# Second layer's MLA gate: tiles 2 to 5 as two more pairs of seven block products, and the products of all pairs collected in PSUM

## The chip, the cores and the metric

The kernel runs on one core of one Trainium2 chip. The metric is the device time of one execution in microseconds; its median is taken over several runs.

## The reference, cut to what matters

A hybrid decoder of two layers works on 512 tokens of width 1024, ahead of which 16 meta tokens are put (528 positions). Each layer projects once, runs two mixers beside each other (causal pooling, latent attention with 8 heads), and gates both:

```python
h = rmsnorm(h_res, norm_gain[l])
proj = h @ w_in[l]
u_pool, z_pool, c_q, c_kv, k_rope, z_mla, g_pool, g_mla = jnp.split(proj, IN_SPLIT_POINTS, axis=-1)
y_pool = (pool_mix(u_pool, pool_w_group[l], pool_scale[l]) * jax.nn.silu(z_pool)) @ pool_w_up[l]
o_mla = mla(c_q, c_kv, k_rope, pos, ...)
y_mla = (o_mla * jax.nn.silu(z_mla)) @ mla_w_up[l]
merged = jax.nn.sigmoid(g_pool) * y_pool + jax.nn.sigmoid(g_mla) * y_mla
h_res = h_res + merged @ w_out[l]
```

The change lies in `g_mla` and `g_pool` of the second layer: two products of 1024 x 1024 weights with the 1024 x 512 normed input. In the second layer the meta tokens are no longer needed there.

## The kernel before, in words

**Layout and matmuls.** Activations lie with features on the 128 partitions and tokens along the row, so an output tile is 128 features by 512 tokens. A float32 product is made as three matmuls (`mm3`, L192, L195, L196): high part of the weights by high part of the activations, high by low, low by high. Weights come in blocks of 128 x 512 (four 128 x 128 weights): `wload` lets SyncE load a block into one of three `raw` buffers (L115), ScalarE makes the high part `whi` (L187) and VectorE the low part `wlo` (L188), of which there are three each. The loads run a few blocks ahead of TensorE. The activations' parts are `hh` and `hl`, one pair for each of the eight slices of 128 features.

**Order.** `plan` is a list of products in program order, and `stream` issues them block by block and stops after every six matmuls. In the attention of a layer each of 8 heads has 4 gaps; `gap` calls `fill(FILL[l], RESERVE[l])`, which issues planned products until a clock of estimated times is FILL ns further on, or until the product named by RESERVE is done; the rest comes after the heads. So the gate products stand between the score, transpose and `p @ v` matmuls of the heads. `after(ns, fn)` issues something once that clock has gone on by ns.

**Gate products of the second layer.** `g_mla` is made as eight plain tiles gm0 to gm7: 8 slices x 3 matmuls of 512 columns, then `ev_gate`: ScalarE's tanh out of PSUM, and for tiles 0 to 5 a store to DRAM (L1069, from ScalarE's queue), since their place in SBUF is still in use; `gates_again` loads them later. `g_pool` is made as four pairs of tiles gp0 to gp3 by `fast`, a scheme of the Strassen kind: two tiles by 512 tokens in seven products of 512 x 128 weights with 256 tokens, each 4 slices x 3 matmuls of 256 columns. Product 1 takes the first tile's weights of the first 512 features, 2 those of the second 512, 4 the second tile's of the second 512; 3, 5, 6 and 7 take sums of weights. `weight_sums` has made these sums in DRAM: for a pair four copies by SyncE (L356, each held behind a matmul that is 14 us old by the clock) and four adding DMAs by GpSimd (L359, behind one of 4 us). For the pool gate that is done in the first layer. The activations' sums and differences for products 4 to 7 are made by `mixed` between the heads (in the names below `cq` for products 6 and 5, `sq` for 7 and 4).

A pair uses four of the PSUM buffers `mm` (there are four in all): products 1 and 2 share one, 7 and 4 one, 5 and 3 one, 6 has its own. A product that shares adds onto what is there. In `fast`, product 1 is copied by ScalarE into half of an `sv` buffer (L632), and five operations of VectorE (L634, L636, L638, L644, L647) combine the products:

```python
order = (1, 6, 7, 5, 2, 4, 3)
...
key = {1: "a", 2: "a", 6: "b", 7: "c", 4: "c", 5: "d", 3: "d"}[p]
...
mm3(ps, w[0][:, c:c + P], w[1][:, c:c + P], xh, xl, k == 0 and p not in (2, 4, 3), k == 3, True)
```

`got_gp` applies the tanh to each of the four half tiles (ScalarE, L657) and VectorE multiplies it onto the pooling branch's `am`. The plan's order is gm0, gm1, gp0, gm2, gp1, gm3, gp2, gm4, gp3, gm5, gm6, gm7; gm6 and gm7 are kept for after the heads.

**Elsewhere.** The rope of the query halves is done by GpSimd and VectorE together (L539 on VectorE, then L541 and L542 on GpSimd). The output stage makes its own seven products with ScalarE copies (L1163).

## Time and profile before

| What | Value |
|---|---|
| runs | 782.56, 782.64, 784.69 us |
| median | 782.64 us |
| profiled execution | 782.78 us, its span 781.0 us |
| TensorE matmul (PE) | 774.8 us, 99% |
| TensorE weight load (PEld) | 712.5 us, 91% |
| VectorE (DVE) | 568.6 us, 73% |
| ScalarE (ACT) | 445.2 us, 57% |
| GpSimd (POOL) | 233.3 us, 30% |
| DMA | 112.92 MB, 145 GB/s on the mean |

Times are in microseconds from the span's start. A row of the timeline gives start, duration, engine, line of the kernel, operation, output and inputs, and the number of instructions; what stands in square brackets is the idle time ahead of it and what ended it. A row of a group gives the count, the busy time, the mean ns of one, and the idle time before them with its releasers. A row of the windows table gives a stretch's length and each engine's busy time in it. The weight loads overlap the matmuls on TensorE.

### The profile page before, as it was taken

To read this page: it belongs to the slowest core of one execution; us is meant where nothing else is said; L and a number is where in the kernel's file an instruction comes from. 1 tells how busy PE (TensorE), PEld (TensorE's weight loads), DVE (VectorE), ACT (ScalarE), POOL (GpSimd) and SP (SyncE) were. 2 spreads that over 40 slices of the span, in tenths; PEclk is the share of its full clock that TensorE was granted. 3 is DMA by queue.
4 is the path that set the end of the run, shared out by engine and by line. 5 is a ranking of instruction groups with operands and counts; after the bars stand their busy time and mean duration, and the time that the engine had idled before them with its cause. 6 is when DMAs were issued, how large, how long until landed. Compare 5 with 4: busy or idle time off the path is not lost.

```text
span 781.0 us, 15326 instructions
## 1 busy us (share of the span) xinstructions
PE 774.8 (99%) x5469; PEld 712.5 (91%) x5469; DVE 568.6 (73%) x1326; ACT 445.2 (57%) x1016; POOL 233.3 (30%) x303
## 2 busy tenths in 40 slices
PE   9999999999999999999999999999999999999998
PEld 9999899999999999999997898887788999988887
DVE  5848787446778876589764477865897888864984
ACT  7645555645566665645564356546667766664462
POOL 1024525103335333211330136221006625440213
PEclk9999999999999999999999999999999999999999
DMA  6242467765746465565662524425556666662655
GB/s 244 82 97 89 124 170 151 179 167 144 156 109 165 115 141 120 155 168 175 168 170 81 98 87 123 132 63 181 141 140 162 174 174 166 176 221 75 209 154 138
DMA packets 65325, 112.92 MB, mean 145 GB/s; under 512 B 10704, under 2 KB 15696, under 8 KB 65248
## 3 DMA queue, kind: packets, MB, share of 16 engines
q1 hardware_dynamic: 55344, 92.18, 40.0%
q0 software_dynamic: 8896, 17.92, 13.0%
q10 hardware_dynamic: 1008, 1.84, 0.6%
q8 instruction: 43, 0.70, 0.4%
q14 instruction: 34, 0.28, 0.1%
HBM read 100.18 MB, written 22.62 MB: 157 GB/s over the span
## 4 chain that ended last, share of the span: by engine, by line
PE 92%; DVE 3%; DMA 2%; ACT 1%; issue 1%; SPq 0%; DVEq 0%; ACTq 0%
PE mm L192 26%; PE mm L196 26%; PE mm L195 26%; PE S L192 3%; PE S L196 2%; PE S L195 2%; PE mm L979 2%; PE o L985 1%; PE o L984 1%; DVE wlo L188 1%; PE S L506 1%; DMA raw<-win 1%; PE mm L408 1%; DMA raw<-wsum 1%; PE mm L465 0%
## 5 line engine op out<-in xcount | busy, mean ns | idle before, releaser
L192 PE MATMUL mm<-hh,whi 128*128 128x264 f32 (+2 forms) x992 | 307.0, 312 | 0.1
L196 PE MATMUL mm<-hh,wlo 128*128 128x264 f32 (+2 forms) x992 | 304.7, 309 | 0.3 <-DVE wlo L188 0.2
L195 PE MATMUL mm<-hl,whi 128*128 128x264 f32 (+2 forms) x992 | 304.4, 308 | 0.0
L188 DVE TENSOR_TENSOR wlo<-raw,whi 128x512 fp32r<-128x512 f32 (+1 forms) x253 | 179.8, 714 | 103.7 <-ACT whi L187 101.2
L187 ACT ACTIVATE whi<-raw 128x512 fp32r<-128x512 f32 (+1 forms) x253 | 154.2, 612 | 166.4 <-PE mm L195 105.0
L192 PEld LDWEIGHTS mm<-hh,whi 128*128 128x128 f32 x992 | 186.6, 189 | 11.0 <-ACT racc L993 0.5
L195 PEld LDWEIGHTS mm<-hl,whi 128*128 128x128 f32 x992 | 187.2, 189 | 8.7
L196 PEld LDWEIGHTS mm<-hh,wlo 128*128 128x128 f32 x992 | 186.2, 188 | 9.4 <-DVE wlo L188 1.1
L922 POOL TENSOR_SCALAR pa<-pa,rs 128x272 f32<-128x272 f32 (+1 forms) x32 | 33.0, 1031 | 103.0 <-DVE rs L941 64.2
L922 POOL TENSOR_SCALAR cq<-cq,rs 128x400 f32<-128x400 f32 (+1 forms) x32 | 52.2, 1631 | 0.0
L192 PE MATMUL mm<-cq,whi 128*128 128x264 f32 (+2 forms) x140 | 43.8, 313 | 0.0
L195 PE MATMUL mm<-cq,whi 128*128 128x264 f32 (+2 forms) x140 | 43.7, 312 | 0.0
L196 PE MATMUL mm<-cq,wlo 128*128 128x264 f32 (+2 forms) x140 | 43.3, 312 | 0.1
L908 DVE CUSTOM_DVE_ANT_0 S<-S,maskw,nqs 128x272 f32<-128x272 f32 (+4 forms) x80 | 38.6, 497 | 5.2 <-PE S L196 4.9
L725 POOL TENSOR_TENSOR racc<-racc,tmp 128x264 f32<-128x264 f32 (+1 forms) x15 | 14.5, 964 | 84.9 <-ACT tmp L724 84.8
L304 DVE TENSOR_TENSOR tl<-mm,th 128x512 fp32r<-128x512 f32 (+1 forms) x64 | 30.0, 482 | 8.0 <-ACT th L303 6.3
L359 POOL DMA_DIRECT2D wsum<-wout x8 | 7.0, 873 | 91.7 <-PE mm L196 77.0
L303 ACT ACTIVATE th<-mm 128x512 fp32r<-128x512 f32 (+1 forms) x64 | 26.2, 432 | 10.2 <-PE mm L979 9.6
L915 ACT ACTIVATE cq<-S,bia 128x400 f32<-128x400 f32 (+2 forms) x48 | 24.4, 513 | 13.2 <-DVE bia L953 8.5
L192 PE MATMUL mm<-u,whi 128*128 128x264 f32 (+1 forms) x96 | 31.3, 326 | 0.0
L196 PE MATMUL mm<-u,wlo 128*128 128x264 f32 (+1 forms) x96 | 30.9, 322 | 0.0
L195 PE MATMUL mm<-kn,whi 128*128 128x264 f32 (+1 forms) x96 | 30.6, 320 | 0.0
(344 smaller groups left out, 1684.2 us busy)
## 6 DMA issues: line engine op xcount, KB each, us to landing
raw<-win SPq DMA_DIRECT2D x139, 256.0 KB, 2.9
raw<-wout SPq DMA_DIRECT2D x22, 256.0 KB, 3.5
bc<-kdr SPq DMA_DIRECT2D x16, 264.0 KB, 4.6
wsum<-wout SPq DMA_DIRECT2D x16, 256.0 KB, 3.5
raw<-wpu SPq DMA_DIRECT2D x16, 256.0 KB, 3.2
wsumgp<-win SPq DMA_DIRECT2D x16, 256.0 KB, 3.3
raw<-wmu SPq DMA_DIRECT2D x16, 256.0 KB, 2.8
raw<-wsumgp SPq DMA_DIRECT2D x16, 256.0 KB, 3.6
```

The source lines that it names most:

```text
L187: act.activation(hi[:, :n], raw[:, :n], AF.Copy)
L188: dve.tensor_sub(lo[:, :n], raw[:, :n], hi[:, :n].bitcast(F32))
L192: first = pe.matmul(out, wh, xh, start=start, stop=False, skip_group_check=more)
L195: pe.matmul(out, wh, xl, start=False, stop=False, skip_group_check=more)
L196: newest[0] = pe.matmul(out, wl, xh, start=False, stop=stop, skip_group_check=more)
L303: act.activation(hi[:, a:b], src, AF.Copy)
L304: dve.tensor_sub(lo[:, a:b], src, hi[:, a:b].bitcast(F32))
L725: self.acc_last = gp.tensor_add(self.acc[:, a:b], self.acc[:, a:b], t[:, :b - a])
L908: dve.tensor_tensor_reduce(out=sv, in0=sv, in1=mask, scale=nqs[:, i, h:h + 1], scalar=3e38, op0=ALU.add, op1=ALU.min, accum_out=bia[:, c:c ...
L915: act.activation(pv, sv, AF.Exp, scale=-1.0, bias=bia[:, i:i + 1], accum_out=rs[:, c:c + 1])
L922: gp.tensor_scalar(pt[i], pt[i], rs[:, i:i + 1], None, op0=ALU.mult)
L979: pe.transpose(tr[:, P * (i - j):P * (i - j + 1)], pt[i][:, NM + P * j:NM + P * (j + 1)], ident)
```

## The change

1. Tiles 2 and 3 of `g_mla` become the pair gq1, tiles 4 and 5 the pair gq2, by `fast` with the evacuation `got_gm`: tanh by halves and a store of each half. `weight_sums` makes their sums in the second layer from the query products on, one of its 16 steps every 4000 ns of the clock (four copies on SyncE and four adding DMAs on GpSimd for each pair).
2. In `fast` the products come in the order 1, 2, 6, 7, 5, 4, 3. Products 1, 6, 5 and 3 add up in one PSUM buffer, 7 and 4 in another, 2 has a third. ScalarE copies the buffer to `sv` after products 1, 6 and 7 (`keep`); VectorE combines once after 2, 5 and 4; 3 is taken from PSUM directly. A pair takes two `sv` buffers. In `mixed` a sign changes with it.
3. The plan's order becomes gm0, gm1, gp0, gq1, gp1, gp2, gq2, gp3, gm6, gm7; FILL of the second layer goes from 2700 to 2640, and RESERVE names gp3 there.

```diff
@@ line 50 of before @@
 G_H, G_CKV, G_CQ, G_QN, G_QR, G_KN, G_KR, G_PS = 0, 8, 10, 16, 17, 18, 19, 20
 N_GAIN = 24
 
-FILL = (2950.0, 2700.0)
-RESERVE = ("gm5", "gm5")
+FILL = (2950.0, 2640.0)
+RESERVE = ("gm5", "gp3")
 LAG = 2000.0
 SPL = 240
 RET = 12500.0
@@ line 335 of before @@
     ksr = [dp.tile([H, T], F32, name=f"ksr{l}") for l in range(DEPTH)]
     kdr = [dp.tile([H, T], F32, name=f"kdr{l}") for l in range(DEPTH)]
 
-    wsum = {n: [dp.tile([P, 4, 512], F32, name=f"wsum{n}{u}") for u in range(k)] for n, k in (("gp", 4), (0, 2), (1, 2))}
+    wsum = {n: [dp.tile([P, 4, 512], F32, name=f"wsum{n}{u}") for u in range(k)] for n, k in (("gp", 4), ("gm", 3), (0, 2), (1, 2))}
     gate = dp.tile([P, 6, SEQ], F32, name="gate")
 
     hbuf = [(slot(f"hh{k}", F32R), slot(f"hl{k}", F32R)) for k in range(8)]
@@ line 344 of before @@
     XH = [(NM, NM + N2), (NM + N2, T)]
     (a, b), (_, c) = XH
 
-    def weight_sums(name, w):
+    def weight_sums(name, w, u0=0):
         def made(u, i):
             a, b = w[2 * u], w[2 * u + 1]
             d = wsum[name][u]
@@ line 358 of before @@
         def add(d, src):
             behind(gp.dma_start(d, src[1], accum_op=ALU.add), earlier(4000))
 
-        for u in range(len(w) // 2):
+        for u in range(u0, len(w) // 2):
             for fn, i in ((copy, 0), (copy, 2), (add, 0), (copy, 1), (add, 2), (add, 1), (copy, 3), (add, 3)):
                 yield lambda fn=fn, u=u, i=i: fn(*made(u, i))
+
+    def wi_(l, t):
+        return win[l, t]
 
     class Layer:
         def __init__(self, l):
@@ line 591 of before @@
             if s == 0:
                 dve.tensor_sub(w[:, b:c], u[:, b:c], w[:, b:c])
                 dve.tensor_sub(u[:, b:c], u[:, a:b], u[:, b:c])
-                dve.tensor_sub(u[:, a:b], u[:, a:b], w[:, b:c])
-                dve.tensor_sub(w[:, a:b], w[:, a:b], u[:, a:b])
+                dve.tensor_sub(u[:, a:b], w[:, b:c], u[:, a:b])
+                dve.tensor_add(w[:, a:b], w[:, a:b], u[:, a:b])
                 return
             if k == 0:
                 self.half = [sqt().bitcast(F32R) for _ in range(14)]
@@ line 605 of before @@
                 split(h_, l_, v, 0, N2)
             self.tt[k] = {6: (th[:, a:b], tl[:, a:b]), 5: (th[:, b:c], tl[:, b:c]), 7: (t3h, t3l), 4: (t4h, t4l)}
 
-        def fast(self, name, a, b, u, got):
-            order = (1, 6, 7, 5, 2, 4, 3)
-            s = wsum["gp"][u]
+        def fast(self, name, wt, kind, u, got):
+            order = (1, 2, 6, 7, 5, 4, 3)
+            a, b, s = wi_(self.l, wt + 2 * u), wi_(self.l, wt + 2 * u + 1), wsum[kind][u]
             src = {1: a[:, 0:512], 2: a[:, 512:1024], 4: b[:, 512:1024], 5: s[:, 0, :], 6: s[:, 1, :], 7: s[:, 2, :],
                    3: s[:, 3, :]}
-            bank = {}
+            bank, kept = {}, {}
+
+            def keep(p, ps):
+                t = kept[p] = self.carry[p == 7][:, HALF * (p == 6):HALF * (p == 6) + N2]
+                act.activation(t, ps, AF.Copy)
 
             def body(i, w):
                 p = order[i]
-                key = {1: "a", 2: "a", 6: "b", 7: "c", 4: "c", 5: "d", 3: "d"}[p]
+                key = {2: "e", 7: "c", 4: "c"}.get(p, "a")
                 if key not in bank:
                     bank[key] = mmt()
                 ps = bank[key][:, :N2]
@@ line 622 of before @@
                 for k in range(4):
                     xh, xl = (x[:, t[0]:t[1]] for x in self.hs[k + o]) if p < 4 else self.tt[k][p]
                     c = P * k
-                    mm3(ps, w[0][:, c:c + P], w[1][:, c:c + P], xh, xl, k == 0 and p not in (2, 4, 3), k == 3, True)
+                    mm3(ps, w[0][:, c:c + P], w[1][:, c:c + P], xh, xl, k == 0 and p in (1, 2, 7), k == 3, True)
                     if k == 1:
                         yield 6 * (N2 / 2.4)
                 if p == 1:
-                    self.part[u] = slot("sv", bufs=2)
-                d, v = self.part[u][:, 0:N2], self.part[u][:, HALF:HALF + N2]
-                if p == 1:
-                    act.activation(d, ps, AF.Copy)
-                elif p == 6:
-                    dve.tensor_sub(d, d, ps)
-                elif p == 7:
-                    dve.tensor_sub(v, ps, d)
+                    self.carry = [slot("sv", bufs=2) for _ in range(2)]
+                if p in (1, 6, 7):
+                    keep(p, ps)
+                elif p == 2:
+                    t = tmp()[:, :N2]
+                    dve.tensor_add(t, ps, kept[1])
+                    got(2 * u, XH[0], t, t)
                 elif p == 5:
-                    dve.tensor_sub(v, v, ps)
-                    got(2 * u + 1, XH[1], v, v)
-                elif p == 2:
-                    got(2 * u, XH[0], ps, tmp()[:, :N2])
+                    t = self.carry[1][:, HALF:HALF + N2]
+                    dve.tensor_sub(t, kept[7], ps)
+                    got(2 * u + 1, XH[1], t, t)
                 elif p == 4:
-                    x = tmp()[:, :N2]
-                    dve.tensor_sub(x, ps, d)
-                    got(2 * u + 1, XH[0], x, x)
+                    t = tmp()[:, :N2]
+                    dve.tensor_sub(t, ps, kept[6])
+                    got(2 * u + 1, XH[0], t, t)
                 else:
-                    dve.tensor_add(d, d, ps)
-                    got(2 * u, XH[1], d, d)
+                    got(2 * u, XH[1], ps, tmp()[:, :N2])
                 if i == len(order) - 1:
                     done.add((self.l, name))
                 yield 6 * (N2 / 2.4)
@@ line 656 of before @@
             am = self.am[m][:, s[0]:s[1]]
             act.activation(t, v, AF.Tanh, scale=0.5)
             dve.scalar_tensor_tensor(out=am, in0=t, scalar=1.0, in1=am, op0=ALU.add, op1=ALU.mult)
+
+        def got_gm(self, m, s, v, t):
+            if self.gms[m] is None:
+                self.gms[m] = slot("ts" if m % 2 else "tc")
+            d = self.gms[m][:, s[0]:s[1]]
+            act.activation(d, v, AF.Tanh, scale=0.5)
+            act.dma_start(gate[:, m, s[0] - NM:s[1] - NM], d)
 
         def window(self, m):
             s = self.us[m]
@@ line 1263 of before @@
                 add(f"zm{m}", wi(MT_ZM + m), D, evac=self.ev_zm(m) if self.last else self.ev_silu(self.zms, "u", m),
                     xs=hs, segs=XS)
             if self.last:
-                for e in ("gm0", "gm1", "gp0", "gm2", "gp1", "gm3", "gp2", "gm4", "gp3", "gm5", "gm6", "gm7"):
+                for e in ("gm0", "gm1", "gp0", "gq1", "gp1", "gp2", "gq2", "gp3", "gm6", "gm7"):
                     m = int(e[2])
                     if e[:2] == "gp":
-                        self.fast(e, wi(MT_GP + 2 * m), wi(MT_GP + 2 * m + 1), m, self.got_gp)
+                        self.fast(e, MT_GP, "gp", m, self.got_gp)
+                    elif e[:2] == "gq":
+                        self.fast(e, MT_GM, "gm", m, self.got_gm)
                     else:
                         add(e, wi(MT_GM + m), D, evac=self.ev_gate(m), xs=hs, segs=XS)
             else:
@@ line 1320 of before @@
                 sums = [*weight_sums(0, [wout[0, m] for m in OUT]), *weight_sums("gp", [win[1, MT_GP + m] for m in range(8)])]
                 for i, fn in enumerate(sums):
                     after(3850 * (i + 1), fn)
+            else:
+                for i, fn in enumerate(weight_sums("gm", [win[1, MT_GM + m] for m in range(6)], 1)):
+                    after(4000 * (i + 1), fn)
             up("qr1")
             for s, (a, b) in enumerate(FULL):
                 a0 = max(a, self.x0)
```

The order of instructions changes only in the second layer. Three places:

On TensorE, before, the start of the pair gp1 among a head's matmuls. `hh_6` to `hh_12` are slices 0 to 3 of the input's high part, `mm_` with a number is a PSUM buffer:

```order
L192 MATMUL mm_8506<-hh_6_132,whi_8447 128x256
...
L196 MATMUL mm_8506<-hh_12_138,wlo_8448 128x256
...
L192 MATMUL mm_8554<-cq_1459_7780,whi_8502 128x256
...
L196 MATMUL mm_8554<-cq_1553_8196,wlo_8503 128x256
L192 MATMUL mm_8574<-sq_7765,whi_8550 128x256
...
L192 MATMUL mm_8506<-hh_14_140,whi_8624 128x256
```

And in the change, at the pair with the same place:

```order
L192 MATMUL mm_8697<-hh_6_135,whi_8638 128x256
...
L196 MATMUL mm_8697<-hh_12_141,wlo_8639 128x256
L192 MATMUL mm_8719<-hh_14_143,whi_8693 128x256
...
L192 MATMUL mm_8697<-cq_1459_7799,whi_8715 128x256
...
L196 MATMUL mm_8697<-cq_1550_8203,wlo_8716 128x256
L192 MATMUL mm_8780<-sq_7784,whi_8757 128x256
...
L192 MATMUL mm_8697<-cq_1459_7799,whi_8776 128x256
```

Before, product 6 opened a buffer of its own (8554) and product 2 came back to that of product 1 (8506) after three others. Now products 6 and 5 come back to product 1's buffer (8697), with one product between each and the one before it on that buffer.

On SyncE, before, the loads ahead of gp1 (`raw` from `win` is a block of weights as they are, from `wsumgp` a block of sums, `wsum` from `wout` a copy for the output stage's sums):

```order
L115 DMA raw_8312<-win 128x512
L115 DMA raw_8341<-wsumgp_123 128x512
L115 DMA raw_8385<-win 128x512
L889 DMA qhl_107<-q_1317_7199 32x512
L889 DMA qhl_108<-q_1318_7200 32x512
L115 DMA raw_8407<-win 128x512
L115 DMA raw_8445<-win 128x512
L115 DMA raw_8500<-wsumgp_124 128x512
```

And in the change, where gq1 and then gp1 follow gp0:

```order
L115 DMA raw_8446<-win 128x512
L900 DMA qhl_107<-q_1317_7208 32x512
L900 DMA qhl_108<-q_1318_7209 32x512
L115 DMA raw_8468<-wsumgm_128 128x512
L115 DMA raw_8525<-wsumgm_128 128x512
L356 DMA wsum_133<-wout 128x512
L115 DMA raw_8544<-wsumgm_128 128x512
L115 DMA raw_8592<-win 128x512
L115 DMA raw_8614<-wsumgm_128 128x512
```

The blocks 8385 and 8407, which served 12 matmuls of 512 columns each, are gone; seven blocks that serve 12 of 256 columns each stand there.

On GpSimd, before, the two rope operations of the query halves (`q_1306`, `q_1319`), with the last operation ahead of them:

```order
L725 TENSOR_TENSOR racc_6059<-racc_6059,tmp_7105 128x512
L541 TENSOR_TENSOR q_1306_7155<-q_1306_7155,tc_103 128x512
L542 TENSOR_TENSOR q_1306_7155<-q_1306_7155,tmp_7161 128x512
L541 TENSOR_TENSOR q_1319_7201<-q_1319_7201,tc_103 128x512
L542 TENSOR_TENSOR q_1319_7201<-q_1319_7201,tmp_7207 128x512
```

And in the change (`wsumgm` are the new sums in DRAM):

```order
L359 DMA wsumgm_128<-win 128x512 x2
L359 DMA wsumgm_128<-wsumgm_128 128x512
L736 TENSOR_TENSOR racc_6062<-racc_6062,tmp_7112 128x512
L544 TENSOR_TENSOR q_1306_7163<-q_1306_7163,tc_103 128x512
L359 DMA wsumgm_128<-wsumgm_128 128x512
L545 TENSOR_TENSOR q_1306_7163<-q_1306_7163,tmp_7169 128x512
L544 TENSOR_TENSOR q_1319_7210<-q_1319_7210,tc_103 128x512
L545 TENSOR_TENSOR q_1319_7210<-q_1319_7210,tmp_7216 128x512
L359 DMA wsumgm_129<-win 128x512 x2
```

Four adding DMAs of the first pair stand ahead of or between these operations, and the second pair's follow them.

## The prediction

> **What bounds the kernel now.** Read first, from the page: the span, TensorE's row, the clock row and the shares of the chain that ended last.
>
> ```profile
> span 781.0 us, 15326 instructions
> PE 774.8 (99%) x5469; PEld 712.5 (91%) x5469; DVE 568.6 (73%) x1326; ACT 445.2 (57%) x1016; POOL 233.3 (30%) x303
> ...
> PEclk9999999999999999999999999999999999999999
> ...
> PE 92%; DVE 3%; DMA 2%; ACT 1%; issue 1%; SPq 0%; DVEq 0%; ACTq 0%
> ```
>
> TensorE is busy for 774.8 of 781.0 us, its clock is granted in full in all 40 slices, and 92% of the chain lies on it. An edit therefore gains what it takes out of TensorE's row of matmuls, less the waits that it puts into that row. The profiled execution took 782.78 us, 1.78 around its span and 0.14 above the median of 782.64; the sum below starts from 782.78, and 0.14 is taken off at its end.
>
> Second, the windows table, for the stages that the edit touches and one that serves as a yardstick.
>
> ```profile
> core 0: us, PE busy (x) PEld busy (x) DVE busy (x) ACT busy (x) POOL busy (x), PEclk, DMA share, GB/s
> 130.00:160.00 30.00, 30.00 (x258) 28.57 (x257) 17.46 (x33) 18.91 (x47) 8.66 (x11) 1.00 0.74 177
> ...
> 497.00:571.00 74.00, 73.90 (x340) 58.24 (x339) 54.42 (x97) 41.34 (x82) 7.62 (x5) 1.00 0.46 133
> 571.00:705.00 134.00, 133.60 (x855) 119.80 (x854) 111.83 (x293) 90.78 (x235) 59.34 (x72) 1.00 0.66 174
> ```
>
> The gate products fill TensorE between the second layer's heads, in 571 to 705: TensorE 133.60 of 134 us, VectorE 111.83 (83%), ScalarE 90.78 (68%). The new weight sums are made in 497 to 571. Nothing of the first layer is touched.
>
> **TensorE's term.** Third, the timeline of TensorE, for the distance between starts of two widths; busy times overlap and don't give it.
>
> ```profile
> 577.09 0.39 PE L192 MATMUL mm<-hh,whi 128*128 128x512 f32 x1
> ...
> 590.03 0.40 PE L196 MATMUL mm<-hh,wlo 128*128 128x512 f32 x1
> ...
> 609.05 0.29 PE L192 MATMUL mm<-hh,whi 128*128 128x256 f32 x1
> ...
> 611.76 0.28 PE L196 MATMUL mm<-cq,wlo 128*128 128x256 f32 x1
> ```
>
> From the first to the second row are 56 steps of 512 columns: 12.94 / 56 = 0.2311 us each. From the third to the fourth are 23 steps of 256 columns: 2.71 / 23 = 0.1178. Tiles 2 to 5 now take 4 tiles x 8 x 3 = 96 of the wide ones, 22.19 us. Two pairs of seven products with 12 narrow matmuls each make 168, 19.79 us. The term is **-2.40 us**. The pool gate's pairs keep their 84 matmuls each; they are only put in another order. FILL lets each of 32 gaps plan 60 ns less; the planned work shrinks too, and what is kept for the end (gm6, gm7) stays the same: 0, with those two tiles as cover.
>
> **Work beside it.** Groups by line, 605 to 705, and one gate store from ScalarE's timeline:
>
> ```profile
> L187 ACT ACTIVATE whi<-raw 128x512 fp32r<-128x512 f32 x40 | 25.2, 630 | 18.3 <-PE mm L195 8.0 <-DMA raw<-win 5.4 <-PE mm L979 2.3
> L657 ACT ACTIVATE tmp<-tmp 128x256 f32<-128x256 f32 x4 | 1.6, 410 | 0.0
> L632 ACT ACTIVATE sv<-mm 128x256 f32<-128x256 f32 x4 | 1.5, 378 | 0.0
> L1067 ACT ACTIVATE ts<-mm 128x512 f32<-128x512 f32 x3 | 1.8, 589 | 0.0
> ...
> L188 DVE TENSOR_TENSOR wlo<-raw,whi 128x512 fp32r<-128x512 f32 x39 | 27.1, 696 | 9.8 <-ACT whi L187 8.9 <-PE mm L979 0.5
> L634 DVE TENSOR_TENSOR sv<-sv,mm 128x256 f32<-128x256 f32 x4 | 1.7, 416 | 0.2 <-PE mm L196 0.2
> ...
> 630.85 0.35 ACTq L1069 DMA_DIRECT2D gate<-tc  x1
> ```
>
> Fourteen weight blocks replace eight. ScalarE gains 6 splits x 0.630, 14 copies out of PSUM x 0.378 (two more in each of four pool pairs, three in each of two new ones), eight half tanhs x 0.410 for four whole ones x 0.589, and four gate stores x 0.35: 3.8 + 5.3 + 0.9 + 1.4 = 11.4 us. VectorE gains 6 x 0.696 and 6 - 8 operations x 0.416: 3.3 us. In 131.6 us ScalarE stands at 78% and VectorE at 88%: both below TensorE, so this costs nothing by itself. If that cover goes, what they deliver late (weights, copies) holds TensorE; the next terms price that.
>
> **Weights (term a).** A load may start when the third block before it has been split, since there are three raw buffers. One slow and one fast round of that loop, from the timelines of all engines:
>
> ```profile
> 629.21 0.68 DVE L188 TENSOR_TENSOR wlo<-raw,whi 128x512 fp32r<-128x512 f32 x1
> 631.35 1.57 SPq L115 DMA_DIRECT2D raw<-win  x2
> 637.12 0.63 ACT L187 ACTIVATE whi<-raw 128x512 fp32r<-128x512 f32 x1 [1.28 <-DMA raw<-win]
> 637.78 0.69 DVE L188 TENSOR_TENSOR wlo<-raw,whi 128x512 fp32r<-128x512 f32 x1 [1.52 <-ACT whi L187]
> 638.53 0.39 PE L196 MATMUL mm<-hh,wlo 128*128 128x256 f32 x1 [0.22 <-DVE wlo L188]
> ...
> 660.90 0.69 DVE L188 TENSOR_TENSOR wlo<-raw,whi 128x512 fp32r<-128x512 f32 x1
> 661.62 2.32 SPq L115 DMA_DIRECT2D raw<-win  x3
> 664.25 0.63 ACT L187 ACTIVATE whi<-raw 128x512 fp32r<-128x512 f32 x1 [0.57 <-DMA raw<-win]
> 665.12 0.68 DVE L188 TENSOR_TENSOR wlo<-raw,whi 128x512 fp32r<-128x512 f32 x1
> ```
>
> The slow round took from 629.89 to 638.47, 8.6 us, and TensorE waited 0.22 for it; the fast one, 661.59 to 665.80, took 4.2. What TensorE leaves for a round comes out of the order of its instructions: the columns between the first use of a block and of the third before it, at 0.456 ns a column (between 0.2311/512 and 0.1178/256), come to a mean of 7.5 us for 43 blocks before and 6.5 us for 50 now, with five below 5 us before and eleven now. This is because two wide blocks (2.8 us of matmuls each) no longer stand between pairs, whose blocks last 1.4 us. I take half of the six new tight places at 0.22: **+0.7**. The ends are 0 and, if the mean round rose to 7.0 us, 14 rounds x 0.5 = 7.
>
> **Copies (term b).** Products 6, 5 and 4 now add onto a bank from which ScalarE must first have copied. The output stage does this already:
>
> ```profile
> 756.51 0.63 ACT L187 ACTIVATE whi<-raw 128x512 fp32r<-128x512 f32 x1 [1.29 <-DMA raw<-wsum]
> 757.05 0.64 ACT L1163 ACTIVATE sv<-S 128x256 f32<-128x256 f32 x2
> ...
> 757.47 0.39 PE L192 MATMUL S<-cq,whi 128*128 128x256 f32 x1 [0.26 <-ACT sv L1163]
> ...
> 763.41 0.39 PE L192 MATMUL S<-cq,whi 128*128 128x256 f32 x1 [0.23 <-ACT sv L1163]
> ```
>
> Two of its six copies held TensorE, 0.26 and 0.23, the first behind a weight split. Behind the waiting matmul stands all of TensorE. A copy needs about 1.3 us: 0.3 for the last matmul, 0.63 if a split is ahead, 0.38 itself. By the order, the cover of the 18 new copies is 1.4 to 1.8 us at five and 2.0 to 3.3 at the others. I take two waits of 0.25: **+0.5**, between 0 and 18 x 0.26 = 4.7.
>
> **GpSimd and the sums (term c).** One of the eight accumulating DMAs is put between the two rope operations:
>
> ```profile
> 523.72 1.81 POOL L541 TENSOR_TENSOR q<-q,tc 128x512 f32<-128x512 f32 x1 [4.97 <-DVE tmp L539]
> 525.61 1.35 POOL L542 TENSOR_TENSOR q<-q,tmp 128x512 f32<-128x512 f32 x1
> ...
> 588.09 0.82 POOL L359 DMA_DIRECT2D wsum<-wout  x1 [8.81 <-PE mm L196]
> ```
>
> It delays the second by 0.82; behind that wait the split of q on ScalarE and a weight split, but the next rope starts only at 528 anyway. **+0.2**, between 0 and 0.82. The eight copies on SyncE wait for matmuls about 14 us old, so they pass. Their transfers are like those in 130 to 160 (DMA share 0.74, TensorE 30.00 of 30): 0 in a stage with 0.46. The seven loads of a pair add 1.5 MB in all to about 23 (134 us x 174 GB/s); that is inside term a.
>
> Gone, on the other side, is the wait at 638.53: **-0.2**. Sum: 782.78 - 2.40 + 0.7 + 0.5 + 0.2 - 0.2 = 781.58, and less 0.14 **781.4 us**.
>
> **The rivals.** *All of it lands.* TensorE's reordered row meets no new wait, and old ones go, as the pool pairs need three VectorE operations instead of five and fewer banks. For it speak the 83% and 68% of the windows row; against it the two waits for copies. 782.64 - 2.40 - 0.2 = 780.0.
>
> *The weight loop becomes the bound*, between 609 and 700. It decides the sign from a mean round of 6.5 us on; at 7.0 it costs 7, and 782.64 - 2.4 + 7 = 787. For it speaks the 8.6 us round, against it the 4.2 us one with all engines as busy.
>
> *The copies become the bound*: all 18 wait as at 757.47, 4.7 us and no gain, 784.9. Against it: 13 covers of 2 us or more.
>
> *Narrow matmuls cost their weight load.*
>
> ```profile
> L192 PEld LDWEIGHTS mm<-hh,whi 128*128 128x128 f32 x992 | 186.6, 189 | 11.0 <-ACT racc L993 0.5
> ```
>
> If a load of 0.189 us set the distance, 168 would take 31.8 instead of 22.2 and the time would be 792.2. The 23 steps of 0.1178 speak against it: loads overlap. The Trainium skill, page "TensorE: Matmul & The Clock Gate", section "Back-to-back issue gap", says that in a stream of load and matmul pairs both set the spacing, and gives 81 ns at 128 columns and 131 at 512; an estimate on the line between them is 98 ns at 256, three quarters of a wide one, by which the change would cost about 7 us. The rows have a half, not three quarters, so the trace decides against the rule here.
>
> That the change doesn't do what it says is excluded by the order: the narrow matmuls are there.
>
> **How the numbers follow.** A measurement tells about 0.3% (2.35 us) from no change: below 780.3 is faster, above 785.0 slower. Chances: forecast 0.49, all lands 0.28, weight loop 0.14, copies 0.08, weight loads 0.01. A little of the forecast lies below 780.3, and half of the copies' case above 785.0. So faster 0.31, same 0.50, slower 0.19. The range goes from 779.0 (the gain and 1.2 of older waits) to 786.0 (a mean round of 6.85 us: 14 x 0.35 = 4.9, beside the 0.7 and the other terms less the gain): it takes in the copies at their bound and leaves out most of the weight loop's case and the edges.
>
> **What would show it.** In the new trace: narrow steps of 0.118 in the gate products (else the last rival); TensorE's waits with the releaser wlo (term a) or the copy line (term b) between 609 and 700, some three and two, under 0.3 us each; the second rope operation near 526.4 and no wait above 0.5 us near 532. The prediction is wrong if these waits pass 2.4 us in sum, if loads take over 6 us to land throughout, or if waits of the stage as it is now vanish by more than 1 us.

## The result, and the profile after

| Kernel | Median (us) | Lowest to highest | Runs |
|---|---|---|---|
| before | 782.78 | 782.06 to 784.69 | 6 |
| changed | 788.89 | 786.49 to 790.47 | 6 |

The ratio is 1.0071, 95% interval 1.0057 to 1.0085: **slower by 5.6 us** (4.5 to 6.7), where 781.4 was forecast with a range of 779.0 to 786.0. Below, "against before" is always (ratio - 1) x 782.7, with the kernel before measured beside each run; so runs of several chips can be set beside each other. The profiled execution of the changed kernel took 788.38 us.

Its page begins so:

```profile
span 786.6 us, 15535 instructions
PE 773.4 (98%) x5541; PEld 712.6 (91%) x5541; DVE 574.7 (73%) x1330; ACT 452.5 (58%) x1040; POOL 237.7 (30%) x311
```

TensorE is busy for 1.4 us less than before, with 72 matmuls more, but the span is 5.6 longer: TensorE now waits for 7.0 us more. The windows table says where most of it lies (columns as in the prediction), first one stage before, then three in the changed kernel:

```profile
705.00:744.00 39.00, 39.00 (x174) 31.73 (x173) 27.55 (x45) 15.88 (x29) 4.42 (x8) 1.00 0.48 152
...
497.00:571.00 74.00, 73.36 (x336) 57.57 (x335) 53.83 (x94) 40.76 (x80) 14.19 (x13) 1.00 0.69 179
571.00:705.00 134.00, 130.63 (x915) 120.39 (x914) 115.06 (x297) 95.96 (x251) 57.02 (x72) 1.00 0.67 180
705.00:744.00 39.00, 37.20 (x167) 29.64 (x166) 26.14 (x44) 16.96 (x32) 3.34 (x6) 1.00 0.44 139
```

In 571 to 705 TensorE idles 3.37 us where it idled 0.40, and in 705 to 744, where it idled not at all, 1.80; in 497 to 571 it is 0.64 for 0.10. VectorE's 115.06 is what the prediction made of it (111.83 + 3.3). The view of waits gives TensorE's own, 497 to 744 (total, times, longest), first its one row before, then the changed kernel's:

```profile
PE mm L196 <- DVE wlo L188: 0.2, 1, 0.2
...
PE o L996 <- DVE tl L304: 1.9, 2, 1.2
PE o L995 <- ACT th L303: 1.5, 3, 0.6
PE mm L192 <- ACT cq L1078: 0.9, 2, 0.6
PE mm L196 <- DVE wlo L188: 0.6, 1, 0.6
PE mm L1001 <- ACT pmr L985: 0.3, 1, 0.3
PE mm L192 <- ACT whi L187: 0.3, 1, 0.3
```

Only 0.9 of the 5.5 us are waits for a weight block (whi, wlo), and none is for one of the new copies (`sv`). Another 0.9 is spent waiting for the tanh of gm6 and gm7 out of PSUM (`cq`, L1078). The largest part, 3.4, is the heads' `p @ v` (`o`), waiting for the high and low parts `th` and `tl` of the transposed probabilities, which ScalarE and VectorE make. What holds those? First ScalarE's waits for blocks of weights in 605 to 720, before:

```profile
ACT whi L187 <- DMA raw<-win: 5.4, 5, 1.8
ACT whi L187 <- DMA raw<-wsumgp: 0.5, 1, 0.5
```

and in the changed kernel:

```profile
ACT whi L187 <- DMA raw<-win: 7.4, 7, 1.8
ACT whi L187 <- DMA raw<-wmu: 3.4, 1, 3.4
ACT whi L187 <- DMA raw<-wsumgm: 2.3, 2, 1.4
ACT whi L187 <- DMA raw<-wsumgp: 1.6, 2, 1.2
```

From 5.9 us in 6 waits to 14.7 in 12 (`wmu` is a block of the product that follows the gate's). One of them in the timelines of all engines:

```profile
627.86 0.38 ACT L620 ACTIVATE sv<-mm 128x256 f32<-128x256 f32 x1
627.88 0.33 SPq L115 DMA_DIRECT2D raw<-wsumgm  x1
627.90 0.38 PE L990 MATMUL mm<-cst,cq 128*128 128x128 f32 x2
629.62 0.63 ACT L187 ACTIVATE whi<-raw 128x512 fp32r<-128x512 f32 x1 [1.37 <-DMA raw<-wsumgm]
630.16 0.36 ACT L303 ACTIVATE th<-mm 128x256 fp32r<-128x256 f32 x1
630.57 0.39 PE L995 MATMUL o<-th,vt 128*128 128x256 f32 x1 [0.58 <-ACT th L303]
```

The two transposes that `th` needs were issued at 627.90. ScalarE stood idle to 629.62 at a weight split, whose block was late, and took `th` behind it; TensorE, at the `p @ v` of that head, waited 0.58. The wait for a gate block came up at a matmul that has nothing to do with the gate. The Trainium skill, page "PSUM — Partial Sum Buffer", section "Engine vs sequencer instructions", says that ScalarE's, VectorE's and GpSimd's queues are strictly first in, first out; this trace agrees: `th` started 0.54 us after the start of the split that stood ahead of it, and 2.26 us after its transposes.

Second, a place where nothing was late:

```profile
658.28 0.69 DVE L188 TENSOR_TENSOR wlo<-raw,whi 128x512 fp32r<-128x512 f32 x1
658.89 0.73 DVE L662 SCALAR_TENSOR_TENSOR xb<-tmp,xb 128x256 f32<-128x256 f32 x1
659.54 0.68 DVE L1023 SCALAR_TENSOR_TENSOR tmp<-tmp,u 128x512 f32<-128x512 f32 x1
660.15 0.51 DVE L919 CUSTOM_DVE_ANT_0 S<-S,maskw,nqs 128x288 f32<-128x288 f32 x1
...
660.75 0.69 DVE L897 TENSOR_TENSOR qhl<-q,qhl 64x512 fp32r<-64x512 f32 x1
661.47 0.70 DVE L188 TENSOR_TENSOR wlo<-raw,whi 128x512 fp32r<-128x512 f32 x1
662.09 1.14 DVE L304 TENSOR_TENSOR tl<-mm,th 128x512 fp32r<-128x512 f32 x2
...
662.82 0.50 PE L996 MATMUL o<-tl,vt 128*128 128x512 f32 x1 [1.18 <-DVE tl L304]
```

VectorE works without a gap, a weight split among the rest, and TensorE waits 1.18 us for what stands last in that row. These are the two theories that the experiments set against each other: **late loads** (an engine stands at a block that has not landed) and **engine load** (ScalarE or VectorE is full just there), and beside them the copies, the sums and FILL.

### The profile page after: what moved, and what is told of

The parts are those of the page before. It is cut to its first block, busy times and chain, and to the rows that moved or that the text cites. A ratio compares the mean times of both kernels' runs of the same rounds, so it can differ in the third digit from the quotient of the medians.

```text
span 786.6 us, 15535 instructions
## 1 busy us (share of the span) xinstructions
PE 773.4 (98%) x5541; PEld 712.6 (91%) x5541; DVE 574.7 (73%) x1330; ACT 452.5 (58%) x1040; POOL 237.7 (30%) x311
## 3 DMA queue, kind: packets, MB, share of 16 engines
q10 hardware_dynamic: 1584, 1.84, 0.7%
## 5 line engine op out<-in xcount | busy, mean ns | idle before, releaser
L192 PE MATMUL mm<-hh,whi 128*128 128x264 f32 (+2 forms) x984 | 300.1, 308 | 1.9 <-DVE u L553 0.8
L196 PE MATMUL mm<-hh,wlo 128*128 128x264 f32 (+2 forms) x984 | 298.5, 306 | 0.1
L195 PE MATMUL mm<-hl,whi 128*128 128x264 f32 (+2 forms) x984 | 297.9, 304 | 0.0
L188 DVE TENSOR_TENSOR wlo<-raw,whi 128x512 fp32r<-128x512 f32 (+1 forms) x259 | 184.9, 717 | 108.7 <-ACT whi L187 104.3
L187 ACT ACTIVATE whi<-raw 128x512 fp32r<-128x512 f32 (+1 forms) x259 | 158.0, 613 | 181.7 <-PE mm L195 101.1
L196 PE MATMUL mm<-cq,wlo 128*128 128x264 f32 (+2 forms) x156 | 48.0, 310 | 0.8 <-DVE wlo L188 0.6
L192 PE MATMUL mm<-cq,whi 128*128 128x264 f32 (+2 forms) x156 | 48.7, 312 | 0.1
L195 PE MATMUL mm<-cq,whi 128*128 128x264 f32 (+2 forms) x156 | 48.2, 309 | 0.0
L919 DVE CUSTOM_DVE_ANT_0 S<-S,maskw,nqs 128x288 f32<-128x288 f32 (+4 forms) x80 | 38.7, 497 | 4.1 <-PE S L196 3.9
L196 PEld LDWEIGHTS mm<-cq,wlo 128*128 128x128 f32 x156 | 29.4, 188 | 3.3 <-DVE wlo L188 1.9
L192 PEld LDWEIGHTS mm<-cq,whi 128*128 128x128 f32 x156 | 29.3, 188 | 1.9 <-ACT sv L620 0.5
L195 PEld LDWEIGHTS mm<-cq,whi 128*128 128x128 f32 x156 | 29.4, 188 | 1.6
```

Of the source, the lines that this page charges most:

```text
L187: act.activation(hi[:, :n], raw[:, :n], AF.Copy)
L188: dve.tensor_sub(lo[:, :n], raw[:, :n], hi[:, :n].bitcast(F32))
L192: first = pe.matmul(out, wh, xh, start=start, stop=False, skip_group_check=more)
L195: pe.matmul(out, wh, xl, start=False, stop=False, skip_group_check=more)
L196: newest[0] = pe.matmul(out, wl, xh, start=False, stop=stop, skip_group_check=more)
L919: dve.tensor_tensor_reduce(out=sv, in0=sv, in1=mask, scale=nqs[:, i, h:h + 1], scalar=3e38, op0=ALU.add, op1=ALU.min, accum_out=bia[:, c:c ...
```

## The experiments

| Run | Median (us) | Against before (us, 95%) |
|---|---|---|
| changed kernel | 788.89 | +5.6 (4.5 to 6.7) |
| copies_only | 785.05 | +2.7 (1.8 to 3.7) |
| pairs_only | 792.83 | +10.6 (8.9 to 12.2) |
| no_loads | 786.17 | +3.8 (2.8 to 4.7) |
| no_sums | 787.98 | +5.3 (4.1 to 6.7) |
| late_reload | 788.97 | +6.7 (5.6 to 7.9) |
| after_fill | 787.72 | +5.2 (4.0 to 6.6) |
| raw4 | 783.00 | +0.7 (0.0 to 1.3) |
| before_raw4 | 780.79 | -1.6 (-2.3 to -1.0) |
| before_raw4_again | 780.54 | -1.9 (-2.7 to -1.0) |
| copies_raw4 | 782.99 | +0.7 (0.0 to 1.4) |
| one_copy_raw4 | 780.94 | -1.8 (-2.6 to -1.0) |
| pairs_raw4 | 786.29 | +3.4 (1.9 to 4.9) |
| raw4_nosums | 782.10 | -0.5 (-1.4 to +0.2) |
| raw4_fill | 781.71 | -1.0 (-1.8 to -0.2) |
| raw4_fill2 | 787.15 | +4.2 (3.1 to 5.3) |
| raw4_early | 780.87 | -1.3 (-2.1 to -0.4) |
| raw4_mix | 781.36 | -1.2 (-2.1 to -0.3) |
| mixform | 782.69 | +0.2 (-0.8 to +1.3) |

**The two halves of the change.** `copies_only` is the changed kernel with the plan of before:

```diff
-FILL = (2950.0, 2640.0)
-RESERVE = ("gm5", "gp3")
+FILL = (2950.0, 2700.0)
+RESERVE = ("gm5", "gm5")
...
-                for e in ("gm0", "gm1", "gp0", "gq1", "gp1", "gp2", "gq2", "gp3", "gm6", "gm7"):
+                for e in ("gm0", "gm1", "gp0", "gm2", "gp1", "gm3", "gp2", "gm4", "gp3", "gm5", "gm6", "gm7"):
...
-            else:
-                for i, fn in enumerate(weight_sums("gm", [win[1, MT_GM + m] for m in range(6)], 1)):
-                    after(4000 * (i + 1), fn)
```

> The pool pairs alone in the new form (order 1, 2, 6, 7, 5, 4, 3, sums in PSUM, three ScalarE copies); tiles 2 to 5 plain and the plan, FILL and RESERVE as before. Theory 'late loads' (ScalarE's queue stands at a weight split whose block is late, and behind it the attention's th): the same blocks are loaded as before, so 782.4 to 783.4. Rival 'copies' (the new copies out of PSUM hold TensorE or ScalarE): four of six pairs carry it, so 786 to 787. Rival 'engine load' (ScalarE and VectorE too full in bursts): eight copies more on ScalarE, eight operations fewer on VectorE, 782.5 to 784.

It measured 785.05, +2.7, outside all three ranges: above late loads (to 783.4) and engine load (to 784), below copies (from 786). The pool pairs' new form is not free. `pairs_only` keeps the plan of the changed kernel and puts the body of `fast` and the signs of `mixed` back to before:

```diff
-            order = (1, 2, 6, 7, 5, 4, 3)
+            order = (1, 6, 7, 5, 2, 4, 3)
...
-                key = {2: "e", 7: "c", 4: "c"}.get(p, "a")
+                key = {1: "a", 2: "a", 6: "b", 7: "c", 4: "c", 5: "d", 3: "d"}[p]
...
-                dve.tensor_sub(u[:, a:b], w[:, b:c], u[:, a:b])
+                dve.tensor_sub(u[:, a:b], u[:, a:b], w[:, b:c])
```

> Tiles 2 to 5 as two pairs, with their sums and the new plan, but all pairs in the old form (order 1, 6, 7, 5, 2, 4, 3, one copy and five VectorE operations). 'Late loads': fourteen short blocks for eight long ones remain, so 788 to 789.5. 'Copies': the cost goes and the 2.4 us of matmuls are gained, 780.5 to 782.5. 'Engine load': VectorE has 12 operations of 0.42 us more than in the changed kernel and ScalarE 12 copies of 0.38 fewer, 787 to 790.

792.83, +10.6: worse than the changed kernel by 5, and above all three ranges. The pairs lose time without the new copies too, and with six pairs the old form is the dearer one. That ends "copies" as the cause of the whole.

**Loads and sums.**

```diff
+            if kind == "gm":
+                src = {p: (p, xb[:, 7, NM:T]) for p in src}
...
-        raw = early.pop(0) if early else fetch(src, n, buf or rawt(), sp)
+        raw = src[1] if isinstance(src, tuple) else early.pop(0) if early else fetch(src, n, buf or rawt(), sp)
```

> The changed kernel, but the 14 blocks of gq1 and gq2 are not loaded: they are split out of a resident buffer (xb of slice 7), so those two pairs multiply by other numbers; ScalarE, VectorE and TensorE do the same work. 'Late loads': most of the 3.4 us of new TensorE waits that go back to a late block goes, 784 to 786. 'Engine load' and 'copies': no change, 788 to 789.5.

```diff
+            if kind == "gm":
+                src.update({5: a[:, 0:512], 6: b[:, 0:512], 7: b[:, 0:512], 3: b[:, 512:1024]})
...
-            else:
-                for i, fn in enumerate(weight_sums("gm", [win[1, MT_GM + m] for m in range(6)], 1)):
-                    after(4000 * (i + 1), fn)
```

> The changed kernel, but the gate's weight sums are not made (no eight copies, no eight adding DMAs); products 3, 5, 6 and 7 of gq1 and gq2 load plain blocks of the weights. If the making of the sums costs only the wait of 0.64 us at 534: 788.2. If its transfers and the rope on GpSimd cost more than that term: below 787.5. 'Late loads' alone: 788.2.

Without the loads of gq1 and gq2, 1.8 us of 5.6 come back, though the intervals overlap a little; other blocks are still late in that kernel (12.2 us of ScalarE's waits are left in 605 to 720: 6.4 for `win`, 3.5 for `wmu`, 2.3 for `wsumgp`). Without the sums 0.3 comes back, which this pair of runs can't tell from nothing; in its trace the wait of 0.64 at 534 is gone.

**A fourth buffer.** This is the test of late loads that changes no work:

```diff
-        return wp.tile([P, 512], F32, tag="raw", name=nm("raw"), bufs=3)
+        return wp.tile([P, 512], F32, tag="raw", name=nm("raw"), bufs=4)
...
-            self.bcs[h] = bc = slot("bc", bufs=3)
+            self.bcs[h] = bc = slot("bc", bufs=2)
```

> The changed kernel with four raw buffers instead of three, so that a load may start one block earlier (a third bc buffer is given up for the room). 'Late loads': with a whole block more of lead, most of the 2.7 us that went without the loads of gq1 and gq2, and of the 2.2 us of the pool pairs' new form, comes back: 784 to 786. 'Engine load': ScalarE and VectorE do the same work, 788 to 789.5.

> The kernel before with the same two buffer numbers, as the control. 'Late loads': it hardly waits for loads, so 782.3 to 783.2. If the buffers help or hurt the kernel everywhere, it moves as much as the changed one does.

The changed kernel gains 4.9 us by it and comes out at 783.00, below the 784 to 786 expected of late loads. The kernel before gains 1.6, where no gain was expected; it had late blocks too, and ScalarE's waits for them in 605 to 720 fall there from 5.9 us to 0.4. In the changed kernel they are now

```profile
ACT whi L187 <- DMA raw<-win: 4.8, 3, 1.9
```

4.8 us for 14.7. So late loads hold about **3.3 us** (4.9 - 1.6) of the 5.6, and 2.3 are left between the two kernels with four buffers each. The edit also takes away one `bc` buffer; what that does by itself no run shows.

**Where the rest lies.** The reloads of the stored gate tiles looked like a cause: all six are issued at 696.6 to 701.3 now, among the last blocks of gm6 and gm7. In `late_reload` they wait for matmuls of gm7, mu0 and mu1.

```diff
+                ins = sp.dma_start(self.gms[m][:, NM:T], gate[:, m, :])
+                if wait:
+                    behind(ins, newest[0])
...
-                self.gates_again()
+                self.gates_again((0, 1), False)
             up("gm7")
             ready()
+            if self.last:
+                self.gates_again((2, 3))
+                up("mu0")
+                self.gates_again((4,))
+                up("mu1")
+                self.gates_again((5,))
```

> The changed kernel with the six reloads of stored gate tiles spread: two where they are, the others held behind matmuls of gm7, mu0 and mu1. Theory 'reload burst': since gq2 and gp3 now end late, all six (1.5 MB) fall between 696.6 and 701.3 onto the last blocks of gm6 and gm7, where before five fell at 685.5 to 688.2; the waits at 708.0, 709.1, 716.9 and 717.6 (0.33, 0.59, 0.62, 0.27) go: 787.0 to 787.7. Otherwise 788.5 to 789.5.

No gain, and three of the four waits are still in its trace (0.58 and 0.27 for `cq`, 0.68 for `th`): that theory fell. The copies, with four buffers in place; `copies_raw4` is `copies_only` with the edit of `raw4`, and `one_copy_raw4` takes away two copies of three a pair:

> The pool pairs alone in the new form (as in copies_only, 785.05), with four raw buffers and two bc buffers. In copies_only ScalarE stood 4.10 us at 617.14 for a block that was issued at 612.68, and the waits of TensorE at 622 to 645 follow it. 'Late loads': 782.5 to 783.5. 'Copies' or 'engine load': 784.5 to 785.5.

```diff
-                if p in (1, 6, 7):
-                    keep(p, ps)
+                if p in (6, 7):
+                    kept[p] = kept[1]
+                elif p == 1:
+                    keep(p, ps)
```

> The pool pairs alone in the new form with four raw buffers (copies_raw4, 782.99, against 780.79 without the new form), but ScalarE copies only product 1 out of PSUM, as before; products 6 and 7 are not copied and VectorE takes product 1's copy in their place, so the pool gate is wrong. The order of the products and the shared PSUM buffers stay. 'Copies' (their time on ScalarE and the waits for them): 780.5 to 781.5. If the product order or the PSUM buffers cost it: 782.5 to 783.5.

`copies_raw4` came out in the range expected of late loads, but the kernel before had gained 1.6 by the same buffers: the new form still costs 2.3 us over `before_raw4` (+0.7 against -1.6), with no wait for a block left on ScalarE in 605 to 720. So its cost isn't late loads. Without eight of its copies **2.5 us** are gone. The product order, the PSUM buffers and the fewer VectorE operations, which stay, together cost nothing that these intervals show. In the trace of `copies_raw4` one place shows how a copy does it, by its place on ScalarE:

```profile
638.03 0.37 ACT L620 ACTIVATE sv<-mm 128x256 f32<-128x256 f32 x1
638.29 0.97 ACT L303 ACTIVATE th<-mm 128x512 fp32r<-128x512 f32 x2
...
639.89 0.68 DVE L304 TENSOR_TENSOR tl<-mm,th 128x512 fp32r<-128x512 f32 x1
...
640.63 0.50 PE L996 MATMUL o<-tl,vt 128*128 128x512 f32 x1 [0.28 <-DVE tl L304]
```

The copy stands ahead of `th`, then comes `tl` on VectorE, and TensorE waits for `tl`. In `one_copy_raw4`, with no copy there, the same two `th` start at 637.75 and TensorE doesn't wait (the two transposes just ahead, of `cq`, started at 636.80 and 636.77 in the two traces):

```profile
637.44 0.41 ACT L663 ACTIVATE tmp<-tmp 128x256 f32<-128x256 f32 x1
637.75 0.97 ACT L303 ACTIVATE th<-mm 128x512 fp32r<-128x512 f32 x2
```

This place gives TensorE 0.28 us of idle time of the 2.5. From 480 us on its waits come to 1.2 us in `copies_raw4` and 0.3 in `one_copy_raw4`; where the copies cost the rest isn't shown.

The other combinations with four buffers: `pairs_raw4` is `pairs_only` with the edit of `raw4`, `raw4_nosums` is `no_sums` with it.

> All six pairs in the old form (pairs_only, 792.83) with four raw buffers. 'Late loads' for the most part: it falls by 6 or more, to 784 to 787, and with it the advantage of the new form in six pairs. 'Engine load' (five VectorE operations a pair where VectorE is fullest): it stays above 788.

+3.4, so six pairs in the old form gain 7.2 from the fourth buffer and still stand 2.7 above the new form. That this is VectorE's load isn't shown: the longest wait of TensorE in this trace, 1.93 us at 659.7, is for an exponential of ScalarE, and behind it the granted clock of TensorE is 0.51 in 660 to 662 and 0.64 in 662 to 664 (more on this below).

> The changed kernel with four raw buffers (783.00), but the gate's weight sums are not made; products 3, 5, 6 and 7 of gq1 and gq2 load plain blocks. With three buffers this took away 0.9 us. If the sums cost that by themselves: 781.9 to 782.4. If that was the late loads: 782.7 to 783.3.

In `raw4_fill` and `after_fill`, and with 2760 in `raw4_fill2`:

```diff
-FILL = (2950.0, 2640.0)
+FILL = (2950.0, 2700.0)
```

> The changed kernel with four raw buffers (783.00) and the second layer's FILL at 2700, as before. The prediction put the smaller FILL at 0: 782.6 to 783.4. If less planned work in a gap leaves the heads' softmax too little time, so that the waits for th and tl come from there: 781.5 to 782.5.

1.2 us less without the sums, whose interval still touches that of `raw4`, and 1.7 less with FILL at 2700, which is clear of it. With three buffers neither shows beyond its interval:

> The changed kernel, three raw buffers, with the second layer's FILL at 2700 as before. With four buffers this edit gave back 1.3 us. If the smaller FILL costs by itself: 787.2 to 788.0. If the late loads cover it with three buffers: 788.4 to 789.4.

It measured 5.2 against 5.6. And FILL is no dial:

> The changed kernel with four raw buffers and FILL 2760. From 2640 to 2700 it gained 1.3 us. If more planned work in a gap keeps giving the softmax time: 780.5 to 781.3. If 2700 was enough, or the work kept for the end becomes too short: 781.6 to 783.

2760 costs 5.2 us over 2700, above both ranges. FILL decides where each product falls among the heads' matmuls, and with it what stands ahead of what in three queues. What it is in 2760 that costs so much isn't settled. The trace is of the fastest of its six runs, 784.26 for a median of 787.15; it has waits of 1.08 and 0.70 at 641 and 642 for a tanh and a copy of ScalarE, and behind them the granted clock is 0.50 in 644 to 646 and 0.68 in 646 to 648.

**A better version.** `raw4_early` is `raw4_fill` with the sums begun earlier, `raw4_mix` has the stores on GpSimd's queue as well:

```diff
             self.norm_sums()
+            if l == 1:
+                for i, fn in enumerate(weight_sums("gm", [win[1, MT_GM + m] for m in range(6)], 1)):
+                    after(4800 * (i + 1), fn)
...
-            else:
-                for i, fn in enumerate(weight_sums("gm", [win[1, MT_GM + m] for m in range(6)], 1)):
-                    after(4000 * (i + 1), fn)
...
-            act.dma_start(gate[:, m, s[0] - NM:s[1] - NM], d)
+            gp.dma_start(gate[:, m, s[0] - NM:s[1] - NM], d)
```

> The changed kernel with four raw buffers and FILL 2700 (781.71), and the gate's weight sums spread from the second layer's start, one step every 4800 ns, instead of from about 497 on every 4000. If the cost of 0.9 us is that of their place (a block that lands late at 534): 780.7 to 781.1. If they cost that wherever their transfers stand: 781.5 to 782.

> raw4_early with the eight half stores of gq1 and gq2 issued by GpSimd instead of ScalarE (eight issues of 0.33 to 0.48 us off ScalarE). 'Engine load' on ScalarE, of which the copies cost 2.1 us: 0.3 to 0.8 us below raw4_early. If issues on ScalarE wait for nothing, or GpSimd's waits delay the heads' scaling there: the same or up to 1 us above.

`raw4_early` beats both kernels of this study, at -1.3, but not `before_raw4`; whether the early sums add to `raw4_fill` (-1.0) is inside the intervals, though no wait at 534 is left in its trace. Stores from GpSimd change nothing that can be measured. Last, all the named costs taken away together: `mixform` is `raw4_early` with the pool pairs in the form of before (`fast_old`, with a sign turned for the new operands):

```diff
-                        self.fast(e, MT_GP, "gp", m, self.got_gp)
+                        self.fast_old(e, MT_GP, "gp", m, self.got_gp)
```

> raw4_early (780.87) with the four pool pairs in the old form (order 1, 6, 7, 5, 2, 4, 3, one ScalarE copy a pair) and only gq1 and gq2 in the new one; four raw buffers, FILL 2700, sums spread early. 'Copies' (2.1 us for the eight of the pool pairs): 778.7 to 779.5, ahead of both kernels and of the kernel before with four buffers. 'Engine load' on VectorE (two operations more in each of four pairs): 780.5 to 783.

> The kernel before with four raw and two bc buffers once more, beside mixform on the same chip: 780.3 to 781.3, so that it can be told whether tiles 2 to 5 as pairs gain anything on top of the buffers. By the 2.4 us of matmuls alone mixform would be 2.4 below it.

+0.2, that is 2.1 above the kernel before with the same buffers, where the matmuls alone would put it 2.4 below. So the costs don't simply add up; a new one takes their place:

```profile
656.09 0.61 ACT L187 ACTIVATE whi<-raw 128x512 fp32r<-128x512 f32 x1
656.62 0.36 ACT L683 ACTIVATE sv<-mm 128x256 f32<-128x256 f32 x1
656.88 0.45 ACT L973 ACTIVATE cq<-S,bia 128x240 f32<-128x240 f32 x1
...
658.15 0.64 ACT L187 ACTIVATE whi<-raw 128x512 fp32r<-128x512 f32 x1
...
658.84 0.38 PE L192 MATMUL mm<-hh,whi 128*128 128x256 f32 x1 [1.84 <-ACT whi L187]
```

Here ScalarE isn't idle: the weight split that TensorE needs stands behind a copy and three exponentials of a head. And something follows the wait that is no queue:

```profile
660.60 0.41 PE L192 MATMUL mm<-sq,whi 128*128 128x256 f32 x1
...
662.30 0.41 PE L196 MATMUL mm<-sq,wlo 128*128 128x256 f32 x1
...
658.00:660.00 2.00, 1.16 (x6) 1.04 (x7) 1.97 (x5) 1.27 (x4) 0.00 (x0) 0.80 0.76 211
660.00:662.00 2.00, 2.00 (x11) 2.00 (x11) 1.93 (x5) 1.13 (x2) 0.95 (x2) 0.50 0.58 196
662.00:664.00 2.00, 2.00 (x16) 1.96 (x15) 1.24 (x3) 0.63 (x1) 2.00 (x3) 0.84 0.10 38
```

Between the first two rows lie 8 steps of 256 columns, 0.2125 us each, where 0.1178 was measured before: TensorE's granted clock (the third column from the right, behind the engines) is 0.50 there. By the three rows this takes up to (0.20 + 0.50 + 0.16) x 2 = 1.7 us, an estimate, beside the wait of 1.84 itself. The traces of `raw4_fill2`, `pairs_raw4`, `pairs_only` (0.50 from 664 to 670) and `no_sums` (0.57 and 0.58 from 770 to 774) have such a stretch too, each during or just behind TensorE's longest waits there, of 1.78 to 3.65 us in sum. The changed kernel's trace, whose longest wait in this part is 1.18, has none while TensorE works, so its 5.6 us aren't this. `raw4_mix` has a wait of 1.77 at 640 and no such stretch, so what brings it on isn't settled. It isn't the whole of `mixform` either: five of its twelve runs have a mean granted clock of 0.997, and the other seven still have a median of 782.29.

## Why the prediction was wrong, step by step

- **"TensorE's term", -2.40: right.** Between two rows of the changed kernel's products, in its timeline,

```profile
642.46 0.33 PE L196 MATMUL mm<-hh,wlo 128*128 128x256 f32 x1
...
646.42 0.28 PE L196 MATMUL mm<-cq,wlo 128*128 128x256 f32 x1
```

  lie 33 steps, 0.1200 us each (0.1178 was used). The rival of the weight loads falls. So does, for these matmuls, the estimate of three quarters from the figures of the Trainium skill, page "TensorE: Matmul & The Clock Gate", section "Back-to-back issue gap": the distance at 256 columns is 0.52 of that at 512.
- **"Both below TensorE, so this costs nothing by itself": the step that failed.** VectorE and ScalarE came out at 86% and 72% of 571 to 705 (115.06 and 95.96 of 134), no fuller than forecast, and yet TensorE waits for them. A share of a stage says nothing on what stands ahead of what in a queue. The prediction looked for late work only at the matmuls that use it, as `wlo` or as a bank not yet copied, and there it is nearly as small as forecast: 0.9 us for blocks. It did not ask who stands behind the late instruction on ScalarE: a head's `th`, and behind that `tl` and `p @ v`, at which 3.4 of TensorE's 5.5 us of waits arose.
- **Term a, +0.7: right mechanism, wrong size and place.** The three-buffer loop is what the rival "the weight loop becomes the bound" had, with 787 to 788.89 measured; the fourth buffer puts the loop's cost in this change at 3.3, not at the rival's 7. That its time came out nearest is luck: copies, sums and FILL make up the difference.
- **Term b, +0.5: wrong mechanism.** The price was sought in TensorE's waits for copies (none in 497 to 744 of the changed kernel); eight copies cost 2.5 with four buffers, and the place at 638 of `copies_raw4` shows one doing so by standing ahead of `th`.
- **Term c, +0.2: too small.** The sums cost about 1.2 with four buffers, where the intervals still touch; in the trace 0.64 of it is one wait for `wlo` at 534. The rope's second operation was held 0.4 (2.31 after the first, 1.89 before), and the next rope came 0.65 later against it, beside the VectorE work ahead of that `wlo`; whether the rope or the block's landing held it wasn't separated.
- **FILL, 0: wrong.** Going from 2700 to 2640 cost 1.7 with four buffers. gm6 and gm7 were no cover, since the edit moves every later product along the heads; through which waits it costs 1.7 isn't shown.
- **The wait at 638.53, -0.2: right.** The changed kernel has no wait for `wlo` in 571 to 705.

With four buffers the pieces -2.4 + 2.5 + 1.2 + 1.7 make 3.0 where 2.3 was measured, and 3.3 for the loads come on top: 6.3 beside 5.6. The 2.5 is of the four pool pairs alone, each piece carries about 1 us of uncertainty, and `mixform` shows that taking them away together doesn't give their sum. What stays open is which queue order would let the 2.4 us through.

A caution on the one profiled execution: of its 5.6 us of span, some 0.9 arose at about 450, ahead of all that the change moves, where a block landed later than in the execution of before; the profiled `before_raw4` has such a wait there too, 1.2 us.

## What to carry to other kernels

When an edit puts work onto an engine that isn't the bound, look at what stands behind each new instruction in that engine's queue, not at the engine's share: a split that waits for its block, or a copy of 0.38 us, delays whatever the queue holds next, and here that was the attention's own chain. When large blocks are replaced by small ones, a load has to be covered by shorter work for the same number of buffers; a fourth buffer was worth 4.9 us to the changed kernel, twice the 2.4 that the edit was to gain, and 1.6 to the old one. Measure that control: beside it, no version of the change had anything to show.

## What the runs showed that was not expected

An edit of 2% in the planned work of a gap (FILL 2640, 2700, 2760) moved the time by -1.7 and then +5.2 us, far beyond the matmuls it moves. And the kernel before, with TensorE at 99%, still had 1.6 us to give for one more buffer. Its waits don't show where: they were 0.2 in 497 to 744, and in `before_raw4` none is left in 480 to 787. What fell is TensorE's busy time, from 774.8 to 770.9 us with the same 5469 matmuls; a busy share of 99% is no measure of how closely they follow each other. TensorE's granted clock also fell to one half for a few us in five of the profiled executions, which made a wait dearer than its own length.
